# A hybrid decoder trunk on one core: the DeltaNet recursion's operands emitted between S5's output quarters, in attention's PSUM banks

## The chip, the cores and the metric

One core of a Trainium2 chip runs the whole kernel in one launch. The metric is the device time of one execution in microseconds (us). The kernel before took 1175.18 us, the median of three runs (1171.71 to 1175.49). TensorE multiplies matrices into PSUM, which has eight banks of 128 partitions by 512 floats; VectorE (DVE in the rows), ScalarE (ACT) and GpSimd (POOL) do the elementwise work, and SyncE starts the loads of weights.

## The reference

Two layers, each of a half-step feed-forward (ffn1), a mixer and a second half-step feed-forward (ffn2), on 272 tokens (16 learned ones and 256 of the input) of 1024 channels, in float32. The mixer projects the normed tokens once and gives the columns to three causal groups, whose normed outputs are joined and projected back:

```
def hybrid_mixer(h, w_in, ...):
    proj = h @ w_in
    sb_q, sb_k, sb_v, dn_qkv, dn_z, dn_b, dn_a, s5_u = split(proj)
    o_sb = rmsnorm(stick_breaking_attention(sb_q, sb_k, sb_v))       # 4 heads of 64
    o_dn = gated_deltanet(dn_qkv, dn_z, dn_b, dn_a, ...)             # 4 heads of 64, normed inside
    o_s5 = rmsnorm(s5_mixer(s5_u, ...))                              # 512 channels
    return concat([o_sb, o_dn, o_s5]) @ w_out
```

The gated DeltaNet is a recursion over chunks; t_inv is the inverse of a unit lower triangular matrix of each chunk, made from the keys and the decays:

```
def step(state, inp):
    v_new = u_i - w_i @ state
    o_i = (q_i * exp(g_i)) @ state + a_i @ v_new       # a_i: q k^T times the decays
    state = state * exp(g_last) + (k_i * exp(g_last - g_i))^T @ v_new
```

S5 is a diagonal state space model over 512 channels. Its output y goes through gelu and a gate, y * sigmoid(y @ w_glu + b).

## The kernel before, in words

Activations lie with channels on the partitions and the 272 tokens along the free axis, eight blocks of 128 channels. Every product of activations with weights is made of three matmuls in the rounded float32 form (mm3, lines 139 to 143): the rounded weights wh times the rounded activations xh, wh times the activations' remainder xl, and the weights' remainder wl times xh. A load of weights brings 512 KB into a raw buffer; ScalarE rounds it into wh (L133) and VectorE subtracts for wl (L136). The loads with a number in ON_POOL have wl made by GpSimd. There are three raw, three wh and two wl buffers, so the wl of one load waits until TensorE is through with the load two before it.

PSUM has four tags, a to d, of two banks each. Streams of weights write a and b, attention writes c (its scores, norms and transposed values) and d (its two outputs, pob), and the recursion writes d.

The mixer's parts are generators and functions. A string, MIX, says in which order their steps are emitted: C, U, Q, K, V and Z are projections (convolution channels, S5's inputs, attention's queries, keys and values, DeltaNet's gate); g the DeltaNet's gates; p, t and y S5's inputs, scans and outputs by quarters of the state groups; i the inverse; a attention; l silu; v attention's values; x the two halves of glu, S5's gate; n and m norms; S the part of the output projection that takes S5's four blocks (S4, S6, S0 and S2 name its columns); o DeltaNet's norm and output. The letter r is a step of dn_rest, the recursion. Its first three steps make the operands: pn, the queries' norms; pl and plt, the query-key products (dn_products); pv and pvt, the transposed values and keys. Then come, for the first chunk pair, pvn (new values) and pS (state and output), for the second pk, pvn and pS, and for the last 16 tokens pkt and pvt2, in two steps.

The string isn't the order on the engines. The framework's scheduler takes the emitted program and its dependences and places each instruction on its engine's queue by its own estimate, with emission as priority; an engine then runs its queue strictly in order. So a wait on one instruction holds everything queued behind it on that engine.

The end of the mixer, which the change and the prediction speak of, is on TensorE: S5's quarters y0 to y3 with V and Z between them; glu's first half and second half, 24 matmuls each (pglu, lines 1305 to 1313); S4 and S6, 24 each (proj); what is left of the recursion; attention's outputs pob (L1275) with a norm pnb (L1281); the transposes po (L1215); then S0. Behind glu's matmuls, ScalarE takes tanh of each block (th), VectorE multiplies (L1318), ScalarE squares (gsq, L1328) and rounds (xh, L1323), VectorE takes the remainder (L1324), and S4 reads both. ScalarE also loads an activation table (L94) behind the last tanh, and copies pvn (L1155) and the last small product's vnt (L1185) for the recursion.

Of the kernel before, what the change touches and what calls it, by code (L numbers as in the profile page):

```python
# [38 lines left out]

MIX = "C2 C3 U0 g U1 g g U2 g g g U3 g Q0 p0 p1 Q1 t0 p2 p3 K0 i t1 K1 a a t2 C0 a a i C1 i t3 a a i C4 i a a i C5 l i " \
      "y0 V0 i y1 V1 i y2 Z0 y3 Z1 v r r r r x r r x r n a r r r r a m S4 S6 o S0 S2"
ON_POOL = (5, 7, 10, 15, 20, 25)
NBUF = (3, 2, 3)
LO_POOL = 5
# [6 lines left out]
def bc(ap, axis, n):  # L53
    return ap.unsqueeze(axis).to_broadcast([*ap.shape[:axis], n, *ap.shape[axis:]])
# [6 lines left out]
class Trunk:  # L61
# [17 lines left out]
    def psum(self, tag, nm):  # L79

        return self.ps.tile([P, 512], F32, tag=tag, name=nm, bufs=2)
# [1002 lines left out]
    def dn_rest(self, qkv):  # L1084
# [6 lines left out]
        quad = [slice(32 * q, 32 * q + 32) for q in range(4)]  # L1091
        unit = lambda c, h: 4 * (h % 2) + 2 * c + h // 2

        pn = self.psum("b", "pn")
        for b in range(2):
            sq = self.cv("sq")
            A.activation(sq, qkv[:, b, :], AF.Square)
# [6 lines left out]
        qn = qkv[:, 0:2]  # L1104
        yield

        AT, ATt = self.E, self.Et
        self.dn_products(qn, AT, ATt, "b")
        yield
        vb, kg = [], []  # L1110
        for c in range(2):
            pv = self.psum("b", "pv")
            for b in range(2):
                PE.transpose(pv[:, b * P:b * P + P], qkv[:, 4 + b, c * P:c * P + P], self.ident)
                PE.transpose(pv[:, 256 + b * P:256 + b * P + P], kn[:, b, c * P:c * P + P], self.ident)
            v, k = tl([P, 4, 64], "vb", 2), tl([P, 4, 64], "kg", 2)
            pvv = pv.rearrange("p (h d) -> p h d", d=64)
            V.tensor_tensor(v, pvv[:, 0:4], bc(bet[:, 4 * c:4 * c + 4], 2, 64), op=ALU.mult)
            V.tensor_tensor(k, pvv[:, 4:8], bc(egl[:, 4 * c:4 * c + 4], 2, 64), op=ALU.mult)
            vb.append(v)  # L1120
            kg.append(k)
        pv = self.psum("b", "pvt")
        for h in range(4):
            PE.matmul(pv[32 * h:32 * h + 32, 0:64], qkv[hsl(h), 4 + h // 2, 256:288], self.ident[hsl(h), hsl(h)], start=True, stop=True)
        vbt = tl([P, 64], "vbt")
# [8 lines left out]
        for c in range(2):  # L1134
            ts = slice(c * P, c * P + P)
            r = vb[c]
# [14 lines left out]
            pv = psum("pvn")  # L1151
            for h in range(4):
                PE.matmul(pv[:, h * 64:h * 64 + 64], TTf[:, unit(c, h), :], r[:, h, :], start=True, stop=True)
            v = v4(qf[:, 1152:1408] if c else ds[:, 256:512])
# [23 lines left out]
        r, v = tl([P, 64], "rt2"), tl([P, 64], "vnt")  # L1178
# [3 lines left out]
        pv = psum("pvt2")  # L1182
# [162 lines left out]
    def mixer(self, l, nxt):  # L1345
# [7 lines left out]
        with ExitStack() as es:  # L1353
# [54 lines left out]
            def w_out_part(x, d0, tag):  # L1408
# [11 lines left out]
                for j in range(2):  # L1420
                    x_, p = self.xT[:, d0 + j, t0:], ps[j][:, :T - t0]
                    if x == "S":
# [11 lines left out]
                         m=lambda: self.rms(self.acc, 4 * 512, 0, self.R5, "b"))  # L1434
            for x in MIX.split():
                if x in chains:
# [53 lines left out]
```

## Time and profile before

| what | value |
|---|---|
| median of three runs | 1175.18 us |
| profiled execution: time, span | 1172.99 us, 1170.9 us |
| TensorE's mean granted clock | 0.983 of full |
| TensorE busy | 1140.0 us, 97% of the span |
| VectorE, ScalarE, GpSimd busy | 73%, 53%, 17% |
| chain that ended last | TensorE 83%, VectorE 10%, GpSimd 2%, ScalarE 2% |

A busy share is an average over the whole span. The mixer of layer 0 stands at about 240 to 392 us, that of layer 1 at about 815 to 970. A timeline row gives the start, the busy time, the engine, the line, the operation with output and inputs, and in brackets how long the engine had been idle and what released it. Matmuls overlap in the pipeline, so what one costs in a stream is the distance of two starts, not its busy time. A window row gives, behind the stretch's length, each engine's busy time with its number of instructions, TensorE's granted clock (1.00 is 2.4 GHz, 0.50 is 1.2 GHz), and the load of the DMA engines.

### The profile page before, as it was taken

To read this page: it belongs to the slowest core of one execution; us is meant where nothing else is said; L and a number is where in the kernel's file an instruction comes from. 1 tells how busy PE (TensorE), PEld (TensorE's weight loads), DVE (VectorE), ACT (ScalarE), POOL (GpSimd) and SP (SyncE) were. 2 spreads that over 40 slices of the span, in tenths; PEclk is the share of its full clock that TensorE was granted. 3 is DMA by queue.
4 is the path that set the end of the run, shared out by engine and by line. 5 is a ranking of instruction groups with operands and counts; after the bars stand their busy time and mean duration, and the time that the engine had idled before them with its cause. 6 is when DMAs were issued, how large, how long until landed. Compare 5 with 4: busy or idle time off the path is not lost.

```text
span 1170.9 us, 23748 instructions
## 1 busy us (share of the span) xinstructions
PE 1140.0 (97%) x9544; PEld 1091.7 (93%) x9544; DVE 858.5 (73%) x1609; ACT 620.5 (53%) x993; POOL 194.0 (17%) x242
## 2 busy tenths in 40 slices
PE   8999999999998999999999999999999989999997
PEld 7999999998896999999999999999988969999985
DVE  7999986599656965565569998756995678666544
ACT  6455465464663654444454555645545737545533
POOL 6312101113310111110202111011141001111100
PEclk9999999999998999999999999999999979999998
DMA  5655544542221455555565565455332216556663
GB/s 186 183 174 174 169 149 151 166 127 60 87 73 55 146 172 173 176 180 163 184 180 168 167 193 163 137 179 156 107 91 74 85 43 198 181 181 189 191 196 109
DMA packets 196858, 173.74 MB, mean 148 GB/s; under 512 B 21300, under 2 KB 193004, under 8 KB 196748
## 3 DMA queue, kind: packets, MB, share of 16 engines
q1 hardware_dynamic: 196732, 172.22, 48.6%
q8 instruction: 75, 1.23, 0.4%
q14 instruction: 35, 0.29, 0.1%
q10 hardware_dynamic: 16, 0.00, 0.0%
HBM read 171.15 MB, written 1.05 MB: 147 GB/s over the span
## 4 chain that ended last, share of the span: by engine, by line
PE 83%; DVE 10%; POOL 2%; ACT 2%; issue 2%; DMA 1%; SPq 0%; ACTq 0%; DVEq 0%; POOLq 0%
PE proj L143 17%; PE proj L142 17%; PE proj L141 17%; PE pd L143 5%; PE pd L142 5%; PE pd L141 5%; PE pd L490 5%; DVE wl L136 2%; PE pY L847 1%; POOL TT L1010 1%; PE pm L780 1%; POOL t L1009 1%; PE pob L1275 1%; PE pY L845 1%; DVE s5z L836 1%
## 5 line engine op out<-in xcount | busy, mean ns | idle before, releaser
L141 PE MATMUL proj<-xh,wh 128*128 128x272 f32 (+1 forms) x1840 | 524.8, 291 | 1.5 <-DVE sy L1424 1.5
L142 PE MATMUL proj<-xl,wh 128*128 128x272 f32 (+1 forms) x1840 | 521.9, 290 | 0.3 <-DVE xl L1222 0.3
L143 PE MATMUL proj<-xh,wl 128*128 128x272 f32 (+1 forms) x1840 | 493.4, 291 | 1.5 <-DVE wl L136 1.2
L133 ACT ACTIVATE wh<-raw 128x1024 fp32r<-128x1024 f32 (+1 forms) x324 | 338.2, 1044 | 291.5 <-PE proj L142 102.2
L136 DVE TENSOR_TENSOR wl<-raw,wh 128x1024 fp32r<-128x1024 f32 (+1 forms) x312 | 378.7, 1214 | 146.2 <-PE pd L143 60.5
L141 PEld LDWEIGHTS proj<-xh,wh 128*128 128x128 f32 x1840 | 348.8, 190 | 4.3 <-DVE sy L1424 2.6
L142 PEld LDWEIGHTS proj<-xl,wh 128*128 128x128 f32 x1840 | 348.3, 189 | 2.4 <-DVE xl L1222 0.5
L143 PEld LDWEIGHTS proj<-xh,wl 128*128 128x128 f32 x1840 | 331.4, 189 | 3.9 <-DVE wl L136 2.9
L432 POOL TENSOR_TENSOR hl<-h,hh 128x272 fp32r<-128x272 f32 (+1 forms) x88 | 80.8, 921 | 452.4 <-ACT hh L431 451.5
L141 PE MATMUL pd<-hh,wh 128*128 128x272 f32 x528 | 149.8, 289 | 0.0
L142 PE MATMUL pd<-hl,wh 128*128 128x272 f32 x528 | 149.5, 288 | 0.0
L143 PE MATMUL pd<-hh,wl 128*128 128x272 f32 x528 | 141.1, 289 | 0.2
L141 PEld LDWEIGHTS pd<-hh,wh 128*128 128x128 f32 x528 | 99.3, 188 | 0.2
L142 PEld LDWEIGHTS pd<-hl,wh 128*128 128x128 f32 x528 | 99.4, 188 | 0.1
L143 PEld LDWEIGHTS pd<-hh,wl 128*128 128x128 f32 x528 | 95.2, 189 | 1.0 <-DVE wl L136 0.9
L104 ACT ACTIVATE g<-g 128x272 f32<-128x272 f32 (+2 forms) x92 | 37.7, 415 | 68.8 <-DVE g L426 68.7
L431 ACT ACTIVATE hh<-h 128x272 fp32r<-128x272 f32 (+1 forms) x88 | 36.3, 419 | 50.7 <-DVE h L430 50.6
L430 DVE TENSOR_TENSOR h<-proj,g 128x272 f32<-128x272 f32 (+1 forms) x88 | 37.8, 434 | 32.3 <-PE proj L143 20.6
L426 DVE TENSOR_TENSOR g<-proj,R 128x272 f32<-128x272 f32 (+1 forms) x88 | 37.5, 431 | 18.3 <-PE proj L143 18.1
L428 DVE TENSOR_TENSOR g<-g,R 128x272 f32<-128x272 f32 (+1 forms) x88 | 37.8, 434 | 12.5 <-ACT g L104 12.2
L136 POOL TENSOR_TENSOR wl<-raw,wh 128x1024 fp32r<-128x1024 f32 x12 | 29.4, 2452 | 97.0 <-PE proj L143 31.9
L373 POOL TENSOR_TENSOR acc<-acc,sq 128x272 f32<-128x272 f32 (+1 forms) x20 | 23.1, 1153 | 91.9 <-ACT sq L367 91.3
(490 smaller groups left out, 1295.4 us busy)
## 6 DMA issues: line engine op xcount, KB each, us to landing
raw<-in_ffn_w_gate_dram SPq DMA_DIRECT2D x88, 512.0 KB, 3.6
raw<-in_ffn_w_up_dram SPq DMA_DIRECT2D x88, 512.0 KB, 3.7
raw<-in_ffn_w_down_dram SPq DMA_DIRECT2D x70, 512.0 KB, 3.5
raw<-in_w_in_dram SPq DMA_DIRECT2D x36, 512.0 KB, 4.3
raw<-in_ffn_w_down_dram SPq DMA_DIRECT2D x24, 384.0 KB, 3.0
raw<-in_w_out_dram SPq DMA_DIRECT2D x16, 512.0 KB, 3.4
raw<-in_s_w_glu_dram SPq DMA_DIRECT2D x4, 512.0 KB, 4.7
xin<-in_x_dram SPq DMA_DIRECT2D x4, 256.0 KB, 6.1
```

The lines of the kernel that those rows point to most:

```text
L104: i = self.nc.scalar.activation(out, in_, func, **k)
L133: nc.scalar.activation(h[:, :n], r[:, :n], AF.Copy)
L136: e.tensor_tensor(l[:, :n], r[:, :n], f32(h[:, :n]), op=ALU.subtract)
L141: mm(p, wh, xh, start=first, stop=False)
L142: mm(p, wh, xl, start=False, stop=False)
L143: mm(p, wl, xh, start=False, stop=last)
L426: V.tensor_tensor(g1, pg[j][:, :N], R, op=ALU.mult)
L428: V.tensor_tensor(g1, g1, R, op=ALU.mult)
L430: V.tensor_tensor(h, pu[j][:, :N], g1, op=ALU.mult)
L431: nc.scalar.activation(hh[:, f, :N], h, AF.Copy)
L432: G.tensor_tensor(hl[:, f, :N], h, f32(hh[:, f, :N]), op=ALU.subtract)
L490: PE.matmul(pd[i][e], x[:, f, ts], w[:, 0, e * 512:e * 512 + 512], start=f == 0 and w is h and x is hh, stop=f == NF - 1 and w is lo)
```

## The change

The string MIX is written anew, and four PSUM tiles of dn_rest's operand steps (pn, dn_products' pl and plt, pv, pvt) take tag c instead of tag b. In the string, the first three r stand before y0, after V0 and after y2, two more behind y3 and Z1, ahead of glu; the rest follow within and behind glu. One i stands before Q0 and most of the others a place or two earlier; v, which was ahead of the first r, now follows the fifth.

```
-MIX = "C2 C3 U0 g U1 g g U2 g g g U3 g Q0 p0 p1 Q1 t0 p2 p3 K0 i t1 K1 a a t2 C0 a a i C1 i t3 a a i C4 i a a i C5 l i " \
-      "y0 V0 i y1 V1 i y2 Z0 y3 Z1 v r r r r x r r x r n a r r r r a m S4 S6 o S0 S2"
+MIX = "C2 C3 U0 g U1 g g U2 g g g U3 g i Q0 p0 p1 Q1 t0 p2 p3 K0 i t1 K1 i a a t2 C0 a i a C1 i t3 a a C4 i a a i C5 l " \
+      "r y0 V0 r i y1 V1 i y2 r Z0 y3 r Z1 r v x r x r r n a r r r a m S4 S6 o S0 S2"
...
-        pn = self.psum("b", "pn")
+        pn = self.psum("c", "pn")
...
-        self.dn_products(qn, AT, ATt, "b")
+        self.dn_products(qn, AT, ATt, "c")
...
-            pv = self.psum("b", "pv")
+            pv = self.psum("c", "pv")
...
-        pv = self.psum("b", "pvt")
+        pv = self.psum("c", "pvt")
```

On TensorE, between the two halves of glu in layer 0 (pglu_4476 and 4477 are the first half's two blocks, pglu_4538 the second half's first), the kernel before has the norms pn and a product pl of the queries:

```order
L142 MATMUL pglu_4477<-xl_95,wh_4480 128x272
L143 MATMUL pglu_4477<-xh_94,wl_4481 128x272
L1099 MATMUL pn_4401<-bd6_385,sq_4402 128x2 x2
L1101 MATMUL pn_4401<-bd6_385,sq_4402 32x1 x2
L882 MATMUL pl_4416<-qkv_3075,kn_3275 128x128 x4
L1099 MATMUL pn_4401<-bd6_385,sq_4408 128x2 x2
L1101 MATMUL pn_4401<-bd6_385,sq_4408 32x1 x2
L141 MATMUL pglu_4538<-xh_94,wh_4542 128x272
L142 MATMUL pglu_4538<-xl_95,wh_4542 128x272
```

In the changed kernel (the first half's blocks are pglu_4487 and 4488) these stand far ahead, and only the last three of pk's matmuls, which were in S6 before, are left between the halves:

```order
L141 MATMUL pglu_4488<-xh_94,wh_4491 128x272
L142 MATMUL pglu_4488<-xl_95,wh_4491 128x272
L143 MATMUL pglu_4488<-xh_94,wl_4492 128x272
L1144 MATMUL pk_4530<-qkv_3075 128x64
L1143 MATMUL pk_4530<-qkv_3075,kn_3275 128x64
L1144 MATMUL pk_4530<-qkv_3075 128x64
L141 MATMUL pglu_4538<-xh_94,wh_4542 128x272
L142 MATMUL pglu_4538<-xl_95,wh_4542 128x272
L143 MATMUL pglu_4538<-xh_94,wl_4543 128x272
```

On TensorE in the kernel before, S4 (proj_4685 and 4686) is broken by the first pvn, by pvt and by the first pS, and the norm pms and S6 (proj_4723) follow:

```order
L143 MATMUL proj_4686<-xh_94,wl_4690 128x272
L1153 MATMUL pvn_4460<-vb_4439,TTf_578 128x64 x4
L141 MATMUL proj_4685<-xh_94,wh_4689 128x272
L141 MATMUL proj_4686<-xh_94,wh_4689 128x272
L1124 MATMUL pvt_4452<-ident_81,qkv_3075 32x64 x4
L142 MATMUL proj_4685<-xl_95,wh_4689 128x272
L143 MATMUL proj_4685<-xh_94,wl_4690 128x272
L142 MATMUL proj_4686<-xl_95,wh_4689 128x272
L143 MATMUL proj_4686<-xh_94,wl_4690 128x272
L1159 MATMUL pS_4512<-ds_4459,kg_4440 64x64 x4
L1161 MATMUL pS_4512<-ds_4459,E_3299 128x64 x4
L385 MATMUL pms_4677<-rs_4467,ones_85 128x272
```

In the changed kernel the first chunk is done long before. S4's last six rows stand behind the second pS and attention's first output pob:

```order
L142 MATMUL proj_4686<-xl_95,wh_4689 128x272
L143 MATMUL proj_4686<-xh_94,wl_4690 128x272
L1159 MATMUL pS_4598<-qkv_3075,kg_4350 64x64 x4
L1161 MATMUL pS_4598<-qkv_3075,E_3299 128x64 x4
L1275 MATMUL pob_4613<-W10_587 64x272
L1276 MATMUL pob_4613<-W10_587,W11_588 64x144
L1277 MATMUL pob_4613<-W10_587,vt_3774 64x16
L1275 MATMUL pob_4613<-W10_587 64x272
L1276 MATMUL pob_4613<-W10_587,W11_588 64x144
L1277 MATMUL pob_4613<-W10_587,vt_3774 64x16
L141 MATMUL proj_4685<-xh_94,wh_4689 128x272
```

ScalarE's queue at the same place before has the table load, the last rounding and square, and then the copy of the first pvn:

```order
L104 ACTIVATE th_4466<-pglu_4539,prm_361 128x272
L94 ACT_TABLE_LOAD
L1323 ACTIVATE xh_94<-s5u_3079,prm_361 128x272
L1328 ACTIVATE gsq_4589<-s5u_3079 128x272
L1155 COPY ds_4459<-pvn_4460 128x256
L133 ACTIVATE wh_4838<-raw_4836 128x1024
L1164 COPY qkv_3075<-pS_4512 128x128
```

Now it is the second pvn whose copy stands right behind the table load, and the square of pob is ahead of the next rounding of weights:

```order
L104 ACTIVATE th_4477<-pglu_4539,prm_361 128x272
L94 ACT_TABLE_LOAD
L1155 COPY qkv_3075<-pvn_4592 128x256
L1323 ACTIVATE xh_94<-s5u_3079,prm_361 128x272
L1328 ACTIVATE gsq_4589<-s5u_3079 128x272
L1279 ACTIVATE sbr_4620<-pob_4613 128x272
L133 ACTIVATE wh_4838<-raw_4836 128x1024
```

Further down ScalarE's queue, the copy of vnt before had only the root of attention's norm ahead of it, with the rounding of the weights wh_4876 five places up:

```order
L104 ACTIVATE rs_4467<-rs_4467 128x272
L133 ACTIVATE wh_4876<-raw_4874 128x1024
L1155 COPY qkv_3075<-pvn_4592 128x256
L1279 ACTIVATE sbr_4606<-pob_4599 128x272
L104 ACTIVATE sbr_4606<-pnb_4609,eps_83 128x272
L104 ACTIVATE sbr_4606<-sbr_4606 128x272
L1185 COPY vnt_4643<-pvt2_4646 128x64
```

Now that rounding stands directly ahead of vnt:

```order
L104 ACTIVATE sbr_4620<-pnb_4623,eps_83 128x272
L104 ACTIVATE sbr_4620<-sbr_4620 128x272
L133 ACTIVATE wh_4876<-raw_4874 128x1024
L1185 COPY vnt_4643<-pvt2_4646 128x64
L1196 ACTIVATE osq_4761<-qkv_3075 128x576
L1286 ACTIVATE xh_94<-sby_4621 128x272
L1279 ACTIVATE sbr_4664<-pob_4657 128x272
```

## Rows read from the trace of the kernel before

**Rows 1.** The page's first part: busy us, share of the span, instructions of each engine.
```profile
PE 1140.0 (97%) x9544; PEld 1091.7 (93%) x9544; DVE 858.5 (73%) x1609; ACT 620.5 (53%) x993; POOL 194.0 (17%) x242
```

**Rows 2.** Busy time by windows; columns PE, PEld, DVE, ACT, (POOL,) PEclk, DMA share, GB/s.
```profile
366.00:369.20 3.20, 1.08 (x32) 0.66 (x32) 2.78 (x9) 0.72 (x3) 0.00 (x0) 0.97 0.00 0
369.20:376.80 7.60, 6.06 (x18) 3.12 (x18) 3.65 (x12) 2.63 (x7) 0.29 (x1) 0.50 0.01 2
955.60:959.40 3.80, 3.79 (x17) 3.79 (x18) 3.71 (x12) 0.95 (x2) 0.00 (x0) 0.50 0.00 0
299.50:302.70 3.20, 0.83 (x73) 0.72 (x73) 2.77 (x7) 0.14 (x1) 0.55 (x3) 1.00 0.00 0
```

**Rows 3.** Timeline of TensorE in layer 0, from S6's end to S0.
```profile
366.84 0.32 PE L1176 MATMUL pkt<-qkv,kn 64*32 64x64 f32 x7 [1.28 <-DVE qkv L1170]
...
367.99 0.31 PE L1184 MATMUL pvt<-rt,TTt 32*32 32x64 f32 x8 [0.70 <-DVE qkv L1180]
368.62 0.31 PE L1188 MATMUL pvt<-vnt,Et 32*32 32x64 f32 x8 [0.32 <-ACT vnt L1185]
369.26 1.17 PE L1275 MATMUL pob<-W 128*64 128x272 f32 x2 [0.32 <-DVE sby L1284]
...
373.62 1.28 PE L1281 MATMUL pnb<-sbr,bd 128*128 128x272 f32 x2 [0.49 <-ACT sbr L1279]
375.46 0.66 PE L1215 MATMUL po<-ident,qkv 128*128 128x128 f32 x2 [0.56 <-DVE qkv L1203]
...
376.76 0.60 PE L141 MATMUL proj<-xh,wh 128*128 128x272 f32 x1 [0.43 <-DVE sy L1424]
```

**Rows 4.** Timeline of TensorE in layer 0, from glu's first half to S6.
```profile
340.99 0.50 PE L1099 MATMUL pn<-bd,sq 128*128 128x2 f32 x4
...
343.36 0.39 PE L141 MATMUL pglu<-xh,wh 128*128 128x272 f32 x1
...
346.32 1.16 PE L882 MATMUL pl<-qkv,kn 64*128 64x128 f32 x8
...
347.61 0.39 PE L142 MATMUL pglu<-xl,wh 128*128 128x272 f32 x1
...
349.37 0.33 PE L1114 MATMUL pv<-ident,qkv 128*128 128x128 f32 x1
...
350.23 0.37 PE L141 MATMUL proj<-xh,wh 128*128 128x272 f32 x1
...
351.64 1.11 PE L1153 MATMUL pvn<-vb,TTf 128*128 128x64 f32 x8
352.55 0.49 PE L141 MATMUL proj<-xh,wh 128*128 128x272 f32 x2
...
353.92 0.45 PE L1159 MATMUL pS<-ds,kg 128*64 128x64 f32 x8
...
355.24 0.68 PE L385 MATMUL pms<-rs,ones 128*128 128x272 f32 x2
...
357.36 0.43 PE L1143 MATMUL pk<-qkv,kn 64*128 64x64 f32 x2
...
358.89 0.40 PE L141 MATMUL proj<-xh,wh 128*128 128x272 f32 x1
```

**Rows 5.** Timeline of ScalarE in layer 0, glu's relay and the copy behind S6.
```profile
340.93 0.49 ACT L104 ACTIVATE th<-pglu,prm 128x272 f32<-128x272 f32 x1 [0.20 <-PE pglu L143]
...
349.90 1.28 ACT L94 ACT_TABLE_LOAD   x1
...
360.58 1.06 ACT L133 ACTIVATE wh<-raw 128x1024 fp32r<-128x1024 f32 x1 [3.67 <-PE proj L142]
```

**Rows 6.** Timeline of VectorE behind glu's first half.
```profile
341.45 2.49 DVE L1318 SCALAR_TENSOR_TENSOR s5u<-th,s5u 128x272 f32<-128x272 f32 x1 [1.15 <-ACT th L104]
...
344.46 0.43 DVE L1318 SCALAR_TENSOR_TENSOR s5u<-th,s5u 128x272 f32<-128x272 f32 x1
```

**Rows 7.** Timeline of GpSimd at the same time.
```profile
341.29 2.35 POOL L136 TENSOR_TENSOR wl<-raw,wh 128x1024 fp32r<-128x1024 f32 x1 [5.46 <-PE pglu L143]
```

## The prediction

> **What bounds the kernel now.** I read the page first. The reader is to see there that TensorE is busy for 1140.0 of 1170.9 us [rows 1]: the kernel is one stream of matmuls, and an edit that only reorders can give back no more than TensorE's pauses and the time it spends at the lower of its two clock levels. Then I cut the span into short windows to find these. In the first layer's mixer they lie behind S6, the last product that needs nothing of the DeltaNet recursion or of attention: from 366.0 to 369.2 TensorE works 1.08 of 3.20 us, and the next 7.6 us run at a granted clock of 0.50, the level of 1.2 GHz [rows 2]. In layer 1 the same: its S0, 3.8 us of matmuls from 955.6 on, stands wholly at 0.50 [rows 2].
>
> Third, TensorE's own instructions in that tail, with what ended each pause [rows 3]: 1.28 us before the last state product pkt, 0.70 and 0.32 in the two small products behind it, 0.32 before attention's second output pob, 0.49 before its norm pnb, 0.56 before the transposes po, 0.43 before S0. That is 4.10 us, all of it a relay between VectorE, ScalarE and TensorE. To it comes the clock. From pob's start at 369.26 to pnb's at 373.62, less the pause of 0.49, are 3.9 us at half speed, so 1.9 more than at full. S0's matmuls cost 0.22 us each (17 in the 3.8 us at 955.6), against 0.13 in a stream at full clock (the 22 of glu between 343.36 and 346.32 [rows 4]): twelve of them, 1.1 us. The tail loses some 7 us per layer, 14 in all. This is the whole prize.
>
> **The change part by part.** No instruction is added or dropped, and the weights are loaded in the same order. What moves is this.
>
> (a) The recursion's operands and its first chunk leave the glu and S4. By start-to-start times [rows 4] they are: pn with the first pl, 340.99 to 343.36, 2.37; the second pl with plt, 346.32 to 347.61, 1.29; both pv, 349.37 to 350.23, 0.86; the first pvn, 351.64 to 352.55, 0.91; the first pS, 353.92 to 355.24, 1.32. Together 6.75 us, and with the small pvt some 7.0. They now stand among S5's output quarters, V and Z, where TensorE has whole streams of weights to work on; it pays for them what it paid before, 7.0 us more there and 7.0 less here. What VectorE does with them lies beside those streams. If that cover fails, TensorE waits for one of the two banks of tag c; the nearest rows are the waits of 0.43 to 0.56 for VectorE in the tail [rows 3], so up to 0.6 per wait and, with two such places, 1.2 per layer. From below: a stream that is broken less often could save a few tenths. Taken: nothing.
>
> (b) pk, 357.36 to 358.89 or 1.53 us [rows 4], moves from S6 into glu's first half. It costs the same there.
>
> So glu's first half ends at 340.99 + 7.0 + 1.5 = 349.5 instead of 340.99, and of what stood between its end and S6 only the rest of glu and S4 are left: 24 + 24 matmuls at 0.13, 6.2 us.
>
> (c) What is late next. From glu's first half to S4's last rows runs a relay on ScalarE and VectorE: tanh, multiply, square, rounding and remainder of each of four blocks. On ScalarE it takes from 340.93 (first tanh) to the end of the table load, 349.90 + 1.28 = 351.18 [rows 5]: 10.2 us, and nothing in that sequence is removed. Its slowest single part stays as well: the multiply behind the first tanh took 2.49 us where the next took 0.43, since GpSimd computed S4's wl from 341.29 to 343.64 [rows 6, 7]. GpSimd starts on that when glu's first half frees the buffer, so the two meet again wherever this half ends. Before, the relay lay under pn and pl, glu's second half, and S4's first rows with pv, pvn, pvt and pS between them, and TensorE hardly waited: S4 was through at 355.24, 14.25 us behind glu's first half. Now TensorE has, behind that half, 3.1 us of glu, 0.9 of the second pvn and 2.3 of S4's first 18 rows, 6.3 us in all. Then stands the second pS, which needs the copy of pvn that ScalarE makes only behind the table load: 10.2 us, and 0.3 for the copy (TensorE waited 0.32 for a like one, vnt [rows 3]). So TensorE waits about 4.2 us here, in two or three pieces, some before S4's first rows. Queued on TensorE behind pS are the first pob and S4's last six rows: 1.3 + 2.0 + 0.8 = 4.1. S4 is through at 349.5 + 10.5 + 4.1 = 364.1.
>
> (d) The tail. Behind it stand S6 (24 at 0.13, 3.1), the norm's sum, pkt and the first pnb (some 1.4, from the steps in [rows 3] less their pauses, pnb's at half). They end at 368.6. The recursion's last operands are ready by then, so the pauses of 1.28 and 0.70 go. But ScalarE now makes a copy of weights of 1.06 us, which waits for S6's last rows as its like did at 360.58 [rows 5], ahead of the copy vnt. That puts the second small product at 368.6 + 1.1 + 0.6 = 370.3 and pob, 0.64 later as before, at 370.9. With pob at full clock (2.0) and the pause of 0.49, pnb starts at 373.4. From there to po, 1.84, and on to S0, 1.30 [rows 3], it is VectorE's roots and multiplies that set the pace, and no clock shortens them. S0 starts at 376.5 against 376.76: 0.2 earlier. If the clock is up then, S0 saves its 1.1 as well.
>
> (e) Attention and the inverse are emitted a place or two earlier. TensorE's longest pauses there are the 2.37 us between 299.5 and 302.7 [rows 2]; they could shrink or grow. Bounds, from that row: 1 us either way per layer. Taken: nothing, as GpSimd's solve, for which they wait, isn't shortened.
>
> (f) The clock. The new pauses in S4 look like those behind S6: about 3.2 us of work in some 7. At 366.0, 1.08 us of work in 3.20 was followed by the low level; at 299.5, 0.83 in 3.20 was not, the granted clock stayed 1.00 [rows 2]. If it falls, the work behind runs at half speed: by the 3.8 us of unbroken matmuls at 0.50 behind 955.6 that loses 1.9; the upper bound is the 4.1 us of pS, pob and S4's last rows all at half speed, 4.1 lost; and S0's 1.1 isn't won. If it doesn't fall it costs nothing. From 0 to 4.1 per layer, then; I take half of the nearer price, 0.9, since the rows show one case of each.
>
> In the Trainium skill, "TensorE: Matmul & The Clock Gate" (A second HAM failure mode: psum-queue depth-cycling) says that frequent short pauses between groups of matmuls make the gate go back and forth. By that sentence the clock falls in S4, and the total is that of the third case below. The window at 366.0 agrees with it, that at 299.5 does not.
>
> **The sum**, per layer: -0.2 (S0's start), -0.5 (half of S0's clock), +0.9 (half of a fall in S4) = +0.2; for both layers +0.4. The profiled execution took 1172.99 us (its span of 1170.9 and 2.1 around it), which makes 1173.4. The median of the runs shown, 1175.18, is 2.2 above that execution; on its scale the forecast is 1175.6.
>
> **The rivals.**
> First, the forecast: glu's relay takes the place of the recursion's. Between -0.2 - 1.1 and +1.3 per layer, so 1172.6 to 1177.8. For it speaks that ScalarE's 10.2 us keep their length and only lose their cover.
>
> Second, faster: the relay gets shorter than I reckon, because VectorE no longer multiplies the recursion's operands in between. If S4 is fed without a pause it ends 4.2 us earlier than under (c), and all of that passes down the tail; half of it is likelier. So 2 to 4 us per layer, and S0's clock with it (1.1): 6 to 10 in all, about 1168. Against it: ScalarE waited for the multiply that GpSimd held up, not for the operands.
>
> Third, slower: the clock falls in S4. Its place is pS, pob and S4's last rows, its price 1.9 to 4.1 per layer, less the 0.2 of (d); so +3.4 to +7.8, about 1180. It decides as soon as TensorE's pauses in S4 come as close together as they did at 366.0.
>
> Fourth: the order on the engines hardly differs, as the list only sets what is emitted, and nothing moves: 1175.2. TensorE's new order differs at all the places named above, so this is nearly excluded.
>
> **How the numbers follow.** A difference under 0.3%, 3.5 us, can't be told from none. Forecast 0.46 and the fourth 0.01: within 0.3%, but for 0.05 at each end that (a) and (e) can carry beyond it. Second 0.28: 0.24 beyond 3.5 us, the rest within. Third 0.25: 0.21 beyond. That makes faster 0.29, slower 0.26, same 0.45. The likeliest case's own range is 1172.6 to 1177.8. For 8 times in 10 the range reaches to the middle of the second and past that of the third: 1168 to 1181.
>
> **What would show it.** In the new trace: no pause before pkt; pauses of together 3 to 5 us between glu's second half and the second pS, the last ended by ScalarE's copy of pvn; vnt behind a copy of weights; S0 of layer 0 within 1 us of 376.5. The granted clock in S4 decides between the first and the third. I am wrong if S4 streams without a pause (then the second), or if a new pause stands among S5's quarters, which I cost at nothing.

## The result, and the profile after

The changed kernel took 1185.83 us, the median of 14 runs (1178.25 to 1195.59); the kernel before took 1173.97 beside it (14 runs, 1169.88 to 1179.59). The ratio is 1.0109, 95% interval 1.0087 to 1.0131: slower, by 1.1%, and 5 us above the forecast's range. On another chip, as a part of the experiments, the same kernel came out at 1.0062 (1.0040 to 1.0083). The profiled execution has a span of 1176.2 us and a mean granted clock of 0.986, and is one of the fastest; the slowest of the 14 took 1195.59 at 0.969. That spread is the clock's: 1178.25 x 0.986 = 1162 and 1195.59 x 0.969 = 1159. Two executions of the experiments, one of streams_between and one of late_z, took over 1.5% more than the fastest of their kernel and are left out of all figures.

I use these two products below for all kernels. Time x (1 - clock) is what the lower level took at most (less where TensorE waited anyway), time x clock is the rest, each as a mean over a kernel's executions. Some 3 us of the first lie behind the last matmul, in the kernel before as well, and cost nothing: from 1171.0 to the end at 1176.2 this profile has 0.50 and no matmul. The two profiles alone would mislead here: that of the changed kernel has the higher clock, 0.986 against 0.983, and only the means over many executions show the loss.

The page's first part, beside [rows 1], busy us and share by engine:

```profile
PE 1143.0 (97%) x9544; PEld 1094.0 (93%) x9544; DVE 849.2 (72%) x1609; ACT 620.1 (53%) x993; POOL 194.6 (17%) x242
```

TensorE does the same 9544 matmuls. Windows of the profile after, columns as in [rows 2]: the row of small products among layer 0's quarters and what follows it, then the tail's stretch at the lower level in two parts, then three such stretches of layer 1.

```profile
313.80:321.00 7.20, 7.20 (x129) 6.54 (x128) 3.79 (x7) 2.23 (x4) 2.06 (x3) 1.00 0.24 73
321.00:324.50 3.50, 3.50 (x18) 3.50 (x18) 0.61 (x2) 1.93 (x5) 0.00 (x0) 0.52 0.02 5
372.25:376.90 4.65, 3.25 (x10) 1.49 (x8) 2.37 (x9) 1.62 (x5) 0.29 (x1) 0.50 0.18 64
376.90:382.50 5.60, 5.56 (x25) 5.56 (x26) 5.51 (x18) 0.95 (x2) 0.00 (x0) 0.51 0.00 0
880.75:887.50 6.75, 6.41 (x64) 5.39 (x68) 4.80 (x10) 1.05 (x2) 0.00 (x0) 0.50 0.30 81
904.75:908.00 3.25, 3.25 (x16) 3.25 (x16) 0.68 (x2) 1.93 (x5) 0.00 (x0) 0.50 0.00 0
942.25:945.50 3.25, 3.25 (x22) 2.91 (x20) 1.18 (x3) 2.50 (x4) 0.00 (x0) 0.50 0.38 130
```

The reader is to see four places at 0.50 where the profile before has 1.00, and that TensorE was not idle before the first of them: from 313.80 to 321.00 it worked 7.20 of 7.20 us (by the profile, which models where matmuls end). Then 3.5 us at 0.52, most of them a stream of weights. Layer 1 has the same at 904.75, one behind the inverse's pause at 880.75 and one in S4 at 942.25. The tail of layer 0 still falls, at 372.25 instead of 369; that of layer 1, at 0.50 from 945.9 to 959.5 before, doesn't.

The row of small matmuls on TensorE that stands before the fall at 321 (timeline as in [rows 3, 4]):

```profile
313.92 1.16 PE L882 MATMUL pl<-qkv,kn 64*128 64x128 f32 x8
...
316.04 0.69 PE L1040 MATMUL px<-T,LT 32*32 32x32 f32 x32
316.66 1.16 PE L882 MATMUL pl<-qkv,kn 64*128 64x128 f32 x8
...
319.41 0.59 PE L1053 MATMUL py<-kb,TT 32*32 32x32 f32 x13
...
321.21 0.57 PE L141 MATMUL proj<-xh,wh 128*128 128x272 f32 x1
```

The last stream of weights ended at 313.9, and the next began at 321.21: 7.3 us of pl, S5's pY, the inverse's px2 and py2, plt. The trace before has shorter rows without a stream at this place, one of 5.05 us at the first quarter (with attention's pz in it), and a stretch earlier in the mixer where this execution of before lost clock and that of after didn't:

```profile
259.50:266.70 7.20, 7.20 (x32) 6.10 (x31) 5.69 (x14) 0.77 (x2) 0.11 (x1) 0.53 0.19 54
305.65:310.70 5.05, 5.05 (x170) 4.42 (x169) 4.73 (x7) 2.73 (x4) 2.35 (x1) 1.00 0.61 179
313.80:317.30 3.50, 3.50 (x98) 3.39 (x97) 2.51 (x4) 3.22 (x8) 0.78 (x2) 1.00 0.11 33
321.20:325.00 3.80, 3.80 (x75) 3.69 (x73) 2.41 (x4) 1.43 (x2) 0.00 (x0) 1.00 0.19 55
```

```profile
259.50:266.70 7.20, 7.20 (x59) 6.62 (x57) 7.20 (x17) 2.49 (x5) 0.11 (x1) 1.00 0.21 60
```

Rows of 3.5 to 5.05 us of small matmuls kept 1.00. The second fence is of after: at 259.5 it had luck, and the first weights behind the first quarter came 2.3 us ahead of the kernel before, on whose times the prediction is built (308.43 for 310.71).

The tail on TensorE, which answers to [rows 3]:

```profile
354.35 0.39 PE L141 MATMUL proj<-xh,wh 128*128 128x272 f32 x1 [0.20 <-ACT xh L1323]
...
356.79 0.40 PE L142 MATMUL proj<-xl,wh 128*128 128x272 f32 x1 [1.09 <-DVE xl L1324]
...
359.24 0.45 PE L1159 MATMUL pS<-qkv,kg 128*64 128x64 f32 x8
...
365.70 0.30 PE L1176 MATMUL pkt<-qkv,kn 64*32 64x64 f32 x2
...
369.95 0.31 PE L1188 MATMUL pvt<-vnt,Et 32*32 32x64 f32 x8 [0.88 <-ACT vnt L1185]
370.68 0.67 PE L1275 MATMUL pob<-W 128*64 128x272 f32 x2 [0.41 <-DVE qkv L1189]
...
373.81 1.27 PE L1281 MATMUL pnb<-sbr,bd 128*128 128x272 f32 x2 [0.49 <-ACT sbr L1279]
375.56 0.69 PE L1215 MATMUL po<-ident,qkv 128*128 128x128 f32 x2 [0.48 <-DVE qkv L1203]
...
376.94 0.60 PE L141 MATMUL proj<-xh,wh 128*128 128x272 f32 x1 [0.48 <-DVE sy L1424]
```

And glu's relay on ScalarE, which answers to [rows 5]:

```profile
348.70 0.47 ACT L104 ACTIVATE th<-pglu,prm 128x272 f32<-128x272 f32 x1
...
357.52 1.28 ACT L94 ACT_TABLE_LOAD   x1
358.81 0.37 ACT L1155 COPY qkv<-pvn 128x256 f32<-128x256 f32 x1
...
368.74 1.06 ACT L133 ACTIVATE wh<-raw 128x1024 fp32r<-128x1024 f32 x1 [0.99 <-PE proj L142]
369.70 0.20 ACT L1185 COPY vnt<-pvt 128x64 f32<-128x64 f32 x1
```

No pause before pkt. The waits in S4 are 0.20, 0.32 and 1.09 us, with some that the busy rows hide: from glu's second half, at 350.02, to the second pS, at 359.24, are 9.2 us for the 6.3 of work that the prediction counted, so 2.9 where it reckoned 4.2. The copy of pvn that pS needs ends at 359.18, behind the table load (357.52 + 1.28), as the order had it. vnt comes behind a copy of weights, 0.88 us late. S0 starts at 376.94 and runs at half speed again.

### The profile page after: what moved, and what is told of

Read it like the earlier page. It is cut to its first block, busy times and chain, and to the rows that moved or that the text cites. A ratio compares the mean times of both kernels' runs of the same rounds, so it can differ in the third digit from the quotient of the medians.

```text
span 1176.2 us, 23746 instructions
## 1 busy us (share of the span) xinstructions
PE 1143.0 (97%) x9544; PEld 1094.0 (93%) x9544; DVE 849.2 (72%) x1609; ACT 620.1 (53%) x993; POOL 194.6 (17%) x242
## 4 chain that ended last, share of the span: by engine, by line
PE 83%; DVE 9%; ACT 2%; POOL 2%; issue 2%; DMA 2%; SPq 0%; ACTq 0%; DVEq 0%; POOLq 0%
PE proj L143 17%; PE proj L141 17%; PE proj L142 17%; PE pd L143 5%; PE pd L142 5%; PE pd L141 5%; PE pd L490 5%; DVE wl L136 2%; PE pY L847 1%; POOL t L1009 1%; PE pm L780 1%; DVE s5z L829 1%; PE pY L845 1%; PE pw L772 1%; ACT wh L133 1%
```

## The experiments

All on the one chip of their group, each against the kernel before on the same chip. The last two columns are the means of time x clock and time x (1 - clock) in us; for the kernel before they are 1155 to 1157 and 17 to 18 on the five chips of the experiments.

| kernel | ratio (95%) | median us | rest | clock |
|---|---|---|---|---|
| changed kernel | 1.0109 (1.0087 to 1.0131) | 1185.8 | 1161.5 | 25.5 |
| the same, another chip | 1.0062 (1.0040 to 1.0083) | 1179.4 | 1161.5 | 19.8 |
| tags_only | 1.0016 (0.9999 to 1.0034) | 1177.5 | 1158.6 | 18.6 |
| i_only | 0.9989 (0.9967 to 1.0011) | 1172.2 | 1153.1 | 20.5 |
| r_only | 1.0168 (1.0139 to 1.0197) | 1194.9 | 1161.0 | 34.1 |
| operands_only | 1.0171 (1.0135 to 1.0207) | 1195.3 | 1153.3 | 40.8 |
| streams_between | 1.0101 (1.0064 to 1.0138) | 1186.6 | 1160.1 | 24.4 |
| late_z | 1.0074 (1.0042 to 1.0106) | 1181.9 | 1154.5 | 28.2 |
| late_z1 | 1.0076 (1.0051 to 1.0102) | 1183.3 | 1154.8 | 28.0 |
| after_no20 | 1.0103 (1.0073 to 1.0134) | 1184.2 | 1161.1 | 22.9 |
| extra_small | 1.0132 (1.0112 to 1.0152) | 1190.3 | 1167.5 | 22.6 |
| extra_wide | 1.0123 (1.0098 to 1.0148) | 1189.3 | 1170.2 | 18.8 |
| sy_b | 1.0062 (1.0042 to 1.0082) | 1181.5 | 1161.1 | 20.9 |
| operands_fill | 0.9991 (0.9973 to 1.0009) | 1172.9 | 1153.8 | 19.5 |
| before_fill | 0.9996 (0.9981 to 1.0012) | 1173.9 | 1154.9 | 19.3 |

**The changed kernel once more.**

> The changed kernel once more, for another execution with a trace beside those already timed (1178 to 1196 us at mean clocks of 0.986 to 0.969). Theory A (the granted clock falls in more places): ratio to before 1.008 to 1.013, and a trace that lies above 1185 us shows, beside the falls in the operands' stretch (layer 0 at about 321, layer 1 at about 905) and in the tail, further stretches of 3 us or more at 0.50, each worth 1.6 to 3 us, that sum up to the difference. Theory B (longer relays and waits, the clock only as a companion): the slower execution has the same falls as the trace at hand, and its additional time is idle time of TensorE.

The profiled execution was again one of the shortest, 1176.95, so no trace of this kernel shows where a long one loses its time. It had other falls than the first: none among layer 0's quarters, one from 895.5 to 909.0 among layer 1's (it began 1.6 us behind the last matmul of a stream), one in S4 of layer 0. The ratio is below what was expected; over the two chips the first part is the same to a tenth and only the second differs.

**The change in its parts**: the tags with the old list, the first line of the list, the second line with the tags.

```
tags_only:  old list; pn, pl, plt, pv, pvt in tag c
i_only:     new first line ("... g i Q0 ... K1 i a a t2 C0 a i a C1 ..."), old second line, tag b
r_only:     old first line, new second line ("r y0 V0 r i y1 V1 i y2 r Z0 y3 r Z1 r v x ..."), tag c
```

> The old list with the operands' PSUM tiles in tag c. Theory A and B: ratio 0.998 to 1.003, since no operand changes its place among the streams by much. A rival, C (attention's banks are the price: pn, pl and pv wait for pz, pnb and pvs, or hold these up): ratio 1.006 to 1.012, with new pauses of TensorE at pl or pvs that end on a VectorE or ScalarE read of a bank of tag c.

> The new list's first line alone (the inverse's steps emitted a place earlier in attention), the operands where they were, tag b. Theory A in the form that the falls come from the operands among S5's quarters: ratio 0.999 to 1.003. Rival D (the earlier inverse makes TensorE stand still longer before px and pz, as at 298 and 880 in the changed kernel's trace, and the clock falls there): ratio 1.004 to 1.010, and the trace shows 0.50 behind px in one layer or both.

> The old first line with the new second line, tag c: the operands and the first chunk go ahead of glu, the inverse's steps in attention stay where they were. Theory A with the operands as the cause: ratio 1.006 to 1.012, falls of the clock among the small matmuls of S5's quarters and pauses in S4 as in the changed kernel. Rival D: ratio 1.000 to 1.004, no fall among the quarters' small matmuls beyond those of the kernel before.

The tags and the inverse's earlier steps can't be told from no change: rivals C and D fall. The recursion's steps ahead of glu are the loss, and without the earlier inverse it is larger, 1.0168. Windows of r_only in layer 0:

```profile
313.60:318.00 4.40, 4.40 (x109) 4.18 (x108) 2.56 (x5) 4.32 (x11) 1.17 (x3) 1.00 0.26 89
318.00:331.75 13.75, 13.75 (x134) 12.96 (x135) 2.75 (x6) 2.38 (x7) 0.21 (x1) 0.50 0.04 12
335.25:345.50 10.25, 10.25 (x55) 9.80 (x55) 1.93 (x5) 1.93 (x5) 0.00 (x0) 0.51 0.13 44
```

TensorE is busy throughout, 4.40 of 4.40 us, before the clock falls for 13.75 us, and again for 10.25. In i_only, which has the inverse of the changed kernel but no operands there, both windows of the quarters keep the full clock:

```profile
305.00:320.00 15.00, 14.89 (x318) 14.19 (x317) 5.37 (x11) 10.79 (x21) 4.52 (x5) 1.00 0.25 72
320.00:340.00 20.00, 20.00 (x188) 19.36 (x188) 9.18 (x16) 12.09 (x27) 3.32 (x2) 1.00 0.26 81
```

**The operands without the first chunk.** The tail of the second line is "Z0 y3 Z1 v r r x r r x r n a ...", so the first pvn and pS stand beside glu as before. The first line is the old one, so the kernel to compare it with is r_only.

> The changed kernel, but with only the operands (pn, pl, pv) among S5's quarters; the first chunk (pvn, pS) is emitted behind glu's start as before, so that TensorE has these matmuls left beside glu's relay. Theory A (clock among the quarters): most of the loss stays, ratio 1.004 to 1.010, with falls of the clock in the quarters of one layer or both. Rival E (the loss is TensorE's pause in S4 under glu's relay): ratio 0.997 to 1.003, as the pause between glu's second half and S6 is under 1 us per layer.

Rival E falls, and the size of the loss was a surprise: 1.0171. Three of the falls among the quarters:

```profile
316.00:329.75 13.75, 13.75 (x137) 12.84 (x137) 2.83 (x8) 3.00 (x7) 0.00 (x0) 0.50 0.01 2
...
903.00:916.75 13.75, 13.75 (x135) 12.74 (x135) 2.75 (x6) 2.86 (x8) 0.60 (x2) 0.50 0.07 24
920.25:930.50 10.25, 10.25 (x56) 9.80 (x56) 2.00 (x6) 1.92 (x5) 0.00 (x0) 0.51 0.16 50
```

13.75 us at 0.50 in each layer. But the rest is 1153, 8 us less than the changed kernel's. The table and the orders on TensorE go together here: kernels whose second pS stands in S4, ahead of its last six rows (the changed kernel, r_only, streams_between, after_no20), have 1160.1 to 1161.5; those with it in S6 (this one, late_z, late_z1) have 1153.3 to 1154.8. That the earlier operands make the tail shorter than before isn't shown: i_only, with the operands where they were, has 1153 as well, and from the first weights behind the first quarter to S0, less half of the time at 0.50, this kernel's profile takes 61.7 and 61.5 us (layers 0 and 1), that of the kernel before 62.2 and 61.0.

**More work among the quarters.** Step D behind y1 and behind y2 of the kernel before, its result unused; in short:

```
+  p = self.psum("c", "dm")
+  extra_small:  12 x PE.matmul(p[:, 128 columns], kn[64 rows, 128], kn[64 rows, 128])
+  extra_wide:   26 x PE.matmul(p[:, :T], xh[:, 0, 0:P], xh[:, 0, :])
```

> The kernel before with needless products added in S5's quarters, after y1 and after y2 of both layers: 12 float32 matmuls each of 64 rows, 128 columns of weights and 128 of keys, like the query-key products pl. By pl's steps (four in 1.1 us) each group costs 3.3 us, 13 us for all four: 1187 us, ratio 1.011, if only their own time counts (theory B). Theory A (small matmuls that keep TensorE busy among S5's and the inverse's small matmuls lower the granted clock): 3 to 10 us above the kernel with the wide ones, ratio 1.014 to 1.020, and a granted clock of 0.50 for 3 us or more in at least one of the two layers' quarters, where the kernel before has none.

> The same as the kernel with the small ones, at the same two places, but each group is 26 matmuls of 128 rows, 128 columns and 272 tokens in the rounded form, 0.126 us each: 3.3 us per group and 13 us in all, ratio 1.011 by theory A and by theory B. Theory A expects no fall of the clock among the quarters here, theory B makes no difference between the two kernels.

By time this doesn't tell them apart: 1.0132 and 1.0123, the intervals overlap, and the first lies below its expectation. Nor do the clock's parts, 22.6 and 18.8: the executions run from 19.0 to 26.2 (four) and from 14.2 to 26.3 (six). The expectation that the wide ones leave the clock up among the quarters failed. Both profiles fell in layer 0, and before the second group of added matmuls had begun: the small ones start at 333.62, the wide ones at 335.02. The row ahead of the fall holds S5's and the inverse's small matmuls alone, without the stream between them that the kernel before had there. The first two lines are of extra_wide, the others of extra_small:

```profile
328.40:331.25 2.85, 2.85 (x41) 2.70 (x39) 1.57 (x2) 1.43 (x2) 0.00 (x0) 1.00 0.01 3
331.25:341.50 10.25, 10.25 (x55) 9.88 (x54) 0.85 (x2) 1.93 (x5) 0.00 (x0) 0.51 0.15 51
326.95:330.05 3.10, 3.10 (x42) 2.95 (x41) 1.95 (x3) 1.42 (x2) 0.00 (x0) 1.00 0.03 11
330.05:343.70 13.65, 13.65 (x69) 12.96 (x69) 0.47 (x2) 1.93 (x5) 0.00 (x0) 0.50 0.12 38
918.10:927.20 9.10, 9.10 (x99) 8.57 (x97) 2.42 (x4) 3.35 (x7) 0.00 (x0) 1.00 0.20 59
```

The last line is the same place in layer 1, with all 12 added products of the second group in it: 9.10 us without a stream, and the clock stayed at 1.00.

**S4's scaled output in a pool of its own.** Meant as a repair of the kernel before, it made it slower.

```
-                        y = self.cv("sy")[:, :T - t0]
+                        y = self.c288("sy")[:, :T - t0]
```

> The kernel before with one tile moved: sy, S4's scaled output, is taken from a pool of six buffers instead of one of three that it shares with attention's sbr and sby. It isn't held back by these then, VectorE frees S4's banks behind the norm's root, and S0 and S2 can run ahead of the recursion's tail. Theory A (the tail's loss is idle time and the clock behind it, some 7 us per layer): 2 to 5 us less per layer, ratio 0.992 to 0.997, and the stretch at 0.50 behind S6 is shorter or gone. A rival (the same chain of waits ends the mixer, whatever stands in between): ratio 0.999 to 1.002, the pauses only move behind S2.

VectorE freed S4's banks early as expected, and TensorE got 38 matmuls of the streams between pk and the second pvn, where it had 12 before. But the recursion stood behind these, and then nothing was left to cover its tail: pauses of 2.27, 0.57, 1.24 and 1.52 us there.

```profile
375.10 0.31 PE L1184 MATMUL pvt<-rt,TTt 32*32 32x64 f32 x8 [2.27 <-DVE qkv L1180]
...
382.30 0.66 PE L1215 MATMUL po<-ident,qkv 128*128 128x128 f32 x2 [0.57 <-DVE qkv L1203]
...
384.41 0.66 PE L1215 MATMUL po<-ident,qkv 128*128 128x128 f32 x2 [1.24 <-DVE dy L1220]
...
386.80 0.59 PE L141 MATMUL proj<-xh,wh 128*128 128x272 f32 x1 [1.52 <-DVE sy L1424]
```

**Other places for the operands.** streams_between has "y0 V0 r i y1 V1 i y2 r Z0 y3 r Z1 v r r x ...", late_z and late_z1 put the second and third r a stream or a quarter later still.

> The kernel with the operands alone ahead of glu (which came out at 1.017), with the three operand steps at other places: behind V0, behind y2 and behind y3 instead of before y0, behind V0 and behind y2. On TensorE they stand ahead of glu as there, 4.5 us per layer, and glu, S4, S6 and the tail have the order of the changed kernel. The difference is what runs between two streams of weights of eight matmuls or more among S5's quarters: at most 4.0 us of small matmuls in a row, by the steps measured, against 6.7 and 5.2 there and in the changed kernel (6.7 and 5.2 in layer 0), and 3.1 in the kernel before. Theory A (the clock falls behind long rows of small matmuls): no fall of the granted clock among the quarters in either layer, ratio 0.998 to 1.006. Rival F (what is moved there costs by itself, wherever it stands, by waits for banks or engines): ratio 1.010 to 1.018.

> The kernel with the operands alone ahead of glu, its second and third operand step a stream later: behind Z0 and behind Z1. TensorE has glu, S4, S6 and the tail in the order of that kernel (first chunk within glu, pk behind it, the second pvn in S4, the second pS in S6), and the products pl stand between Z0's and Z1's streams. Two parts by the mean over executions of time x granted clock and time x (1 - clock), so far: before 1156 + 18, operands alone 1153 + 41, the kernel with other places for them 1161 + 25, the changed kernel 1161 + 20 to 25. If the two parts come from two places (S4's order sets the first, what runs among the quarters the second), this one has 1152 to 1156 + 17 to 24, a ratio of 0.996 to 1.003. If the second part comes with the operands' being early at all, it has 30 or more, a ratio above 1.008.

> As the one before, but the products pl a quarter later still, behind y3, so that both operand steps have Z1's stream around them and pv stands in glu's first half, as the products did before the change. By two parts from two places: 1152 to 1156 + 16 to 22, ratio 0.995 to 1.001, no fall of the clock between the inverse's last product and glu. If being early costs by itself: between 1.003 and 1.010.

streams_between has 16 us less in the clock's part than operands_only, but that is still 7 above the kernel before. These three kernels also have the changed kernel's first line, where operands_only has the old one, so a part of the 16 us can be the inverse's place: it is 20 to 25 us in the changed kernel and 34 in r_only, which differ by that line alone. Falls are there, behind a row of 3.75 us and another, both ahead of the first product pl at 329.96:

```profile
311.50:315.25 3.75, 3.75 (x104) 3.63 (x102) 2.47 (x5) 3.43 (x8) 1.27 (x4) 0.98 0.19 48
315.25:322.00 6.75, 6.75 (x58) 6.44 (x57) 0.43 (x1) 1.92 (x5) 0.11 (x1) 0.50 0.15 53
328.75:339.00 10.25, 10.25 (x61) 9.25 (x61) 1.99 (x4) 1.92 (x5) 0.00 (x0) 0.50 0.05 19
```

The rows weren't as short as planned: in layer 1 the first takes 5.6 us from 903.87, at 1.00, where 4.0 was to be the most. (Its rest is 1160, as the scheduler gave it S4's order of the changed kernel.) late_z and late_z1 have the rest that was expected, 1154.5 and 1154.8, and 28 us on the clock, which was not: late_z lies between its two expectations, late_z1 comes out as if being early cost by itself. Some of late_z's executions have none of it: it ran from 1173.49 at 0.984 to 1190.05 at 0.969, and the profile is of the first. late_z1's fall at 319 came behind a row of small matmuls that holds little but pn more than the row before px2 in the kernel before:

```profile
316.00:319.00 3.00, 3.00 (x97) 2.88 (x97) 2.47 (x5) 2.95 (x6) 0.73 (x2) 1.00 0.04 12
319.00:327.00 8.00, 8.00 (x83) 7.66 (x85) 0.43 (x1) 2.98 (x8) 0.66 (x3) 0.57 0.19 63
```

So the length of a row without a stream doesn't by itself decide it; late_z's profile has the same row, 5.6 us long in both layers, at 1.00. And late_z1's profile has four falls among the quarters (at 319.4, 333.0, 903.0 and 916.7), all of them ahead of pl, which comes at 342.38 and 925.00: the query-key products need not be there for the clock to fall.

**glu's relay without the held-up multiply**: 20 is taken out of ON_POOL.

> The changed kernel with S4's wl made by VectorE instead of GpSimd, so that the multiply behind glu's first tanh isn't held up (0.43 instead of 2.5 us) but VectorE has 1.2 us more to do. The part of the theory that says that glu's relay now sets TensorE's pause ahead of S4's end: the pause between glu's second half and the second pS gets 0.5 to 1.5 us shorter per layer and S6 ends earlier by as much; the time 0 to 3 us below the changed kernel, ratio 1.004 to 1.010. If something else sets that pause, it stays within 0.3 us of what it is, and VectorE's 1.2 us make the kernel no faster.

The multiply took 0.44 us in the changed kernel's profiles already, since GpSimd came 0.2 us too late to meet it (349.42, the multiply at 349.21), against (c), by which the two meet again. There another VectorE instruction took longer beside GpSimd, the sum L1149: 1.66 us, and 0.42 here. From pvn behind glu to the second pS:

```profile
357.62 1.00 PE L1153 MATMUL pvn<-ds,TTf 128*128 128x64 f32 x8
...
363.08 0.45 PE L1159 MATMUL pS<-qkv,kg 128*64 128x64 f32 x8
```

5.46 us, against 353.14 to 359.24, 6.10, in the changed kernel: 0.64 shorter, as expected, and not seen in the time.

**The query-key products left out.**

```
+            if fill:
+                PE.matmul(p, self.identb, bc(self.identb, 1, 4), start=True, stop=True)
-            for c in range(2):
+            for c in range(0 if fill else 2):
```

> The kernel with the operands alone ahead of glu, with the query-key products left out: of each group of four float32 matmuls for pl only one bfloat16 matmul of 512 columns of an identity remains, so that the scores of the DeltaNet chunks are not computed. Beside its control (the kernel before with the same left out) it keeps pn, plt and pv among the quarters and every wait of the operands, but has 1.7 us less per layer of float32 matmuls there. If it is the mass of these matmuls among the quarters that lowers the clock, time x (1 - clock) falls from 41 to 20 to 32 us and the ratio to the control is 1.002 to 1.010. If it is the new order (what the operands push aside, their waits), 36 to 45 us stay and the ratio to the control is 1.013 to 1.019.

> The control: the kernel before with the same query-key products left out, between the halves of glu and in its second half. Time 0.5 to 4 us less than the kernel before, as pl's matmuls there covered glu's relay; time x (1 - clock) within 3 us of 18.

This is the clearest pair. Sixteen float32 matmuls less over both layers (some 4 us by pl's steps, less the fill) take operands_only from 1.0171 to 0.9991 of the kernel before, some 21 us, all of it off the clock's part, 40.8 to 19.5, which is then that of its control. The expectation for the products had been 20 to 32, with 1.002 or more against the control. The quarters, V, Z and glu's start keep the full clock in both layers:

```profile
305.00:352.50 47.50, 47.47 (x682) 44.26 (x681) 24.23 (x43) 29.26 (x59) 7.92 (x7) 1.00 0.24 74
888.00:953.00 65.00, 61.82 (x813) 56.29 (x812) 39.17 (x75) 39.23 (x75) 6.11 (x6) 1.00 0.26 81
```

With pn, plt, pv, their waits and the earlier recursion in place, the kernel is as fast as its control. So in this order the loss comes and goes with the query-key products. It isn't shown that they lower the clock themselves: with less to do for pl, the scheduler also put 16 matmuls of a stream between px2 and py2, so the products and the order that they force are only taken away together, and the falls ahead of pl in late_z1 and ahead of the added products in extra_small speak for the order.

No version beat the kernel before: i_only (0.9989) and operands_fill (0.9991, with the products left out) can't be told from it.

## Why the prediction was wrong

The forecast was no change, 1175.6; it came out at 1185.8.

**Step (a) failed**: "it pays for them what it paid before, 7.0 us more there and 7.0 less here", with 1.2 us per layer as the worst case and nothing taken. The direct 7.0 is about right: in the second profile, which has no fall among layer 0's quarters, the weights behind the first quarter come 2.2 us earlier than in the kernel before (308.49 for 310.71) and Z1 ends 4.0 later (341.3 for 337.3): 6.2 us, with 5.7 (all but pS) moved in between. But the clock isn't in that sum. (f) looked for its fall behind pauses only, and only in S4. The row that would have warned of it lay in the trace before, 259.50 to 266.70 at 0.53 with TensorE busy for 7.20 of 7.20 us among the gates' small products. The operands' steps among the quarters, with the order that they force, bring this about there. Over the whole execution the clock's part grew by 2 to 8 us in the changed kernel (19.8 and 25.5 against 17 to 18), 16 in r_only, 23 in operands_only.

**The forecast's mechanism, (c) and (d), was right in place and short in size.** glu's relay took the place of the recursion's, pS waits for the copy behind the table load, vnt for a copy of weights, and each came within 0.8 us of its predicted time (glu's first half 350.0 for 349.5, pS 359.2 for 360.0, pob 370.7 for 370.9, pnb 373.8 for 373.4, S0 376.9 for 376.5). But the 2.3 us that this execution was ahead behind the first quarter are in there, so relative to that all are 1.5 to 2.8 us late, 1.7 of it the fall at 321. That was luck. From the first weights behind the first quarter to S0 the kernel before takes 66.1 and 65.9 us, the changed kernel 68.5 and 68.4, in the second profile 67.3 and 71.5; 0.2 less was forecast. Less half of the time at 0.50 it is 62.2 and 61.0 before and 64.4 to 65.6 in the changed kernel, 2 to 4 us more per layer; over executions the part that isn't the clock is 5 us for both layers (1161.5 against 1156.6). The table points to S4 for it: kernels with the second pS in S6 have 7 us less. The profiles bear this out in part (operands_only 61.7 and 61.5, but late_z 63.8 and 62.6), and what in S4's order costs it isn't shown. It isn't the held-up multiply, (c)'s slowest part: in the changed kernel this took 0.44 us.

**Step (f)**: half of a fall in S4 was taken, and of the two profiles each has one in one layer of two. The size, 1.7 us, is near the 1.9 of which half was taken. That agrees with the Trainium skill's sentence on short pauses ("TensorE: Matmul & The Clock Gate", A second HAM failure mode: psum-queue depth-cycling) in two of the four cases. The price for the kind of fall that did the harm was too low: 3.8 us behind 955.6 were only the end of 13.6 at 0.50, and falls of that length came among the quarters.

```profile
945.90:959.50 13.60, 11.09 (x66) 7.44 (x55) 9.25 (x27) 3.81 (x10) 0.29 (x1) 0.50 0.00 0
```

S0's clock was held in one layer of two in both profiles, as half was taken.

**The third rival** was the right kind (slower, by the clock) with the wrong place: it said S4, and its price of 3.4 to 7.8 us would not have held the 11.9.

**Step (e)** was right by i_only: within the interval of no change.

What stays open: what in these rows lowers the clock (that the matmuls are float32, that they are narrow, or that no stream breaks the row), why the same kernel in the same order has the falls in one execution or layer and not in the next, and whether a place for the operands exists that keeps both 1153 and 18.

## What to carry to other kernels

Moving small float32 matmuls together can cost a kernel that is bound by TensorE twice: their own time, which moves with them, and the clock of what follows, here for 3 to 14 us. Look in the trace before for stretches where the granted clock is low although TensorE is busy, and see what ran there. Mean time x (1 - clock) over all executions tells this part from the waits, where one profiled execution, here mostly one of the shortest, does not. And before a chain is freed, see which other chain lay under the same work: here glu's relay lay under the recursion's products, and freeing one uncovered the other.

## What was not expected of the hardware

The granted clock fell to half with TensorE busy all the time: 13.75 us at 0.50 behind 4.40 us of small products (r_only), 10.25 us behind 2.85 (extra_wide), while rows of 3.5 and 3.8 us kept it (before), and one of 9.10 us (extra_small). Busy is meant by the profile, which models where matmuls end. Executions of one kernel on one chip differ by little else: late_z from 1173.49 us at 0.984 to 1190.05 at 0.969, by time x clock 1155 and 1153.
